# A float32 decoder trunk on one core: low halves of the feed-forward forms by accumulating DMAs, three more seven-product pairs per layer, one in each GLA projection, four pieces of work later

## The chip, the core and the metric

The kernel runs on one core of one Trainium2 chip. The engines named below are TensorE (PE, matrix products), VectorE (DVE), ScalarE (ACT), GpSimd (POOL) and SyncE (SP); each works through its own instructions in order, and DMA queues are started from SP, POOL and ACT. The metric is the device time of one execution in microseconds (us). A profiled execution takes 2254.6 us, of which its trace spans 2252.8.

## The reference, cut to what matters

256 tokens of width 2048, all float32. Two layers; each has a token mixer with a cross-attention beside it, an output projection and a feed-forward part:

```
mem_n = _rmsnorm(mem, norm_mem)
for layer in range(2):
    hn = _rmsnorm(h, norm_mix[layer])
    y, xq = mixer(hn, w_in)              # layer 0: HGRN2, layer 1: gated linear attention (GLA)
    xa = _memory_attention(xq, mem_n, w_mem_kv[layer])
    h = h + concatenate([y, xa]) @ w_out[layer]
    hn = _rmsnorm(h, norm_ffn[layer])
    gate, up = split(hn @ w_gate_up[layer])
    h = h + (silu(gate) * up) @ w_down[layer]
return _rmsnorm(h, norm_final)
```

## The kernel before, in words

**Halves.** Every float32 factor is split into a high half, rounded to the matmul's format, and a low half, the rest. A product of two blocks is three matmuls: high by high, high by low, low by high. The weights come from HBM into a buffer `raw`, one pair of rows of blocks at a time (256 rows, four quarters of up to 512 columns). ACT casts them into the high half and DVE subtracts that from the buffer for the low half; both halves lie in a tile `parts87c` and the like (the number counts the weight pairs, the letter the split in it; in output projection some are called `parts_0` and `parts_2`).

**Plain, seven and H pairs.** A pair joins a 2 by 2 grid of x blocks (two row blocks, two token halves of 128) with a 2 by 2 grid of weight blocks. Plain, it is eight block products, 24 matmuls, and two splits of 1024 columns each. With a Strassen-Winograd scheme it is seven products, 21 matmuls ("S"): sums of the weight quarters are formed in `raw` and split as well (function `seven`; splits a to d of 512, 1024, 1024 and 1024 columns), and sums of the x blocks ("s", "d0", "u", "z") are needed beside them. If it is fed, one of the quarter sums is made by an accumulating DMA of POOL (line 444 for `raw`, lines 428 and 429 for a tile `T` beside it). "H" and "O" are other forms with eight products, which need fewer or no sums: H splits 1024, 1024 and 512 columns and forms one difference of 512. A plan such as `0-1S2S3-` lists pairs and kinds in their order; KINDS lists the kinds of the eight pairs of a feed-forward block, its first entry for block 0 ("block one" below).

**Forms of x.** In the feed-forward part class `Forms` (line 371) makes the x side of a pair once per layer: PE transposes four blocks of h (`tp_hf`), ACT writes them with the gain into `g`, a buffer of a ring of two (tag "stg"; `hf_7g` for pair 7), DVE adds up the further forms in `g`, and `parts()` (line 402) makes the halves `hf_7h` and `hf_7l` (one tile `hf_6hl` for pair 6): an ACT copy and a DVE subtraction, 1024 columns for eight forms. Pair 7 is of kind "B": when that is done, a ninth form is written into g[:, 4] and split likewise. Class `More` makes the further forms for output projection and down projection from halves that exist (tiles `y_6g`, `y_6m`).

**The stages.** The memory tokens are projected to keys and values for both layers (`m0p`, `m1p`; scaling by the memory norm behind the first); then per layer the mixer, output projection (its first quarter alone, `wo`; quarters two and three by plan OUT; its last quarter alone), and eleven feed-forward blocks of 512 columns (`f_p`) with the down projection (`fd`) between them. GLA works in two halves (`pr` 0 and 1); each first projects keys and queries (`gk0p`, 384 columns wide, plan "------S-"), which ACT scales (`gsk`, `gsq`) and PE transposes (`tgk`, `tgq`), then gates and values (`gg00p`).

**What sets the order.** Small work (transposes, attention, scores) waits in a list; `later(...)` appends pieces, and one piece is taken out at marks between the matmuls of a projection, so that `None` in the list moves what follows by one mark. A scheduler then lists the instructions of each engine when the program is built; on the chip each engine keeps to its list. One helper line (L151) issues nearly all instructions, so the profile's rows are told apart by tiles.

Of the kernel before, what the change touches and what calls it, by code (L numbers as in the profile page):

```python
# [9 lines left out]
F32 = mybir.dt.float32  # L10
# [3 lines left out]
AF = mybir.ActivationFunctionType  # L14
# [26 lines left out]
def trunk_kernel(ctx: ExitStack, tc: tile.TileContext, x, mem, norm_mix, norm_ffn, norm_mem,  # L41
# [210 lines left out]
    def later(*pieces):  # L252
        pending.extend(pieces)
# [119 lines left out]
    class Forms:  # L373
# [20 lines left out]
        def put(self, ps, gains):  # L394

            g = work.tile([P, 8, P], F32, tag="stg", name=f"{self.name}g", bufs=2)
            for k in range(2):
                ac.activation(out=g[:, 2 * k:2 * k + 2, :], in_=ps[:, 2 * k * P:(2 * k + 2) * P].rearrange(
                    "p (a t) -> p a t", t=P), func=AF.Copy, scale=gains[k])
            tt = ve.tensor_tensor  # L400

            def parts(i, j, n):
                ac.copy(out=self.h[:, i:i + n, :], in_=g[:, j:j + n, :])
                tt(out=self.l[:, i:i + n, :], in0=g[:, j:j + n, :], in1=self.h[:, i:i + n, :].bitcast(F32), op=ALU.subtract)

            if self.kind == "O":
                tt(out=g[:, 4:6, :], in0=g[:, 1:3, :], in1=g[:, 0:4:3, :], op=ALU.subtract)
                parts(0, 0, 6)
                return
            tt(out=g[:, 4:6, :], in0=g[:, 3:0:-2, :], in1=g[:, 0:1, :].broadcast_to([P, 2, P]), op=ALU.subtract)  # L410
            ve.scalar_tensor_tensor(out=g[:, 6, :], in0=g[:, 3, :], scalar=-1.0, in1=g[:, 5, :],
                                    op0=ALU.mult, op1=ALU.subtract)
            tt(out=g[:, 7, :], in0=g[:, 2, :], in1=g[:, 6, :], op=ALU.add)
            parts(0, 0, 8)
            if self.kind == "B":
                tt(out=g[:, 4, :], in0=g[:, 2, :], in1=g[:, 3, :], op=ALU.subtract)
                parts(8, 4, 1)
# [256 lines left out]

    def h_quad(hq, q, gain, ss, name, queue=later, sevens=SEVEN):

# [11 lines left out]

        queue(turn)

# [85 lines left out]
    for l in range(2):  # L776
# [4 lines left out]
        project_two(memq["pairs"], MEM[l], w_mem_kv[l], 0, XA, XA, f"m{l}",  # L781
                    lambda: [lambda t: ks[:, t, :], lambda t: vm[l][:, t, :]], prep=prep_mem if l == 0 else None)
        if l == 0:
# [5 lines left out]
            for q in range(NQ):  # L789

                h_quad(hq, q, g_mix[0], ss, "hx", later if q > 1 else first_turns.append)
        for d in (ks, vm[l]):
            for t in range(NT):
                ac.activation(out=d[:, t, :], in_=d[:, t, :], func=AF.Copy, scale=rm[:, t:t + 1])

# [4 lines left out]

        later(turn_keys)

# [4 lines left out]
    def attention(l, ps, r, yq):  # L807
# [42 lines left out]
        def mix():  # L850
            quad = yq[3] = Quad("tq", f"y{l}_3")
            for j in range(2):
# [7 lines left out]

        later(turn_queries, None, lambda: softmax(0), lambda: softmax(1), None,
              lambda: turn_probs(0), lambda: turn_probs(1), mix)
# [204 lines left out]
    def gla_pair(w, pr, dec, decay, hq, r, yq):  # L1067
# [40 lines left out]
        def give():  # L1108
            for name in "kq":
# [3 lines left out]

        project_two(hq["pairs"], ("------S-", "------S-")[pr], w, kw + pr * 2 * DK, pr * 2 * DK, 2 * DK, f"gk{pr}", give,
                    lambda ps: ps.rearrange("p (a c) -> p a c", c=DK), fed=False)
# [5 lines left out]
        if pr == 0:  # L1121
            scores[5:5] = [lambda: decay(1), None]
        later(None, None, turn_k, turn_q, None, None, *scores)
        GLA = (("-----SS-", "-----SS-"), ("-----SS-", "-----SS-"))
# [71 lines left out]

    KINDS = ("SHHSHOSO", "HHHSSOSO", "SHHSSOSO", "SSHSSOHS", "SSSSSOSS")

# [112 lines left out]

    OUT = "4-5-2-0S6S7-3S1-"

# [3 lines left out]
    for l in range(2):  # L1317
# [33 lines left out]
        if l == 0:  # L1351
            hq = {}
            ffn(0, hq2, r2, lambda n: h_quad(hq, n, g_mix[1], ss, "hm1_", sevens=2))
            scale = lambda ss=ss: h_scale(ss, "rm1", True)
# [79 lines left out]
```

## Time and profile before

| | |
|---|---|
| Median of 3 runs | 2254.84 us (2254.82 to 2255.8) |
| The profiled execution | 2254.6 us |
| Its span in the trace | 2252.8 us |
| Busy: PE, DVE, ACT, POOL | 2238.6, 2031.5, 1452.8, 280.4 us |
| Granted TensorE clock, mean | 0.999 |
| DMA queue of POOL (software) | 25632 packets, 50.87 MB, 13.0% of 16 engines |
| DMA queue of SP (hardware) | 228547 packets, 420.21 MB, 55.5% |

The two times are to be kept apart: the profiled execution is 1.8 us longer than the span that its trace covers, and durations read from the trace belong to that one execution. A busy share is a mean over stages with different limits; what a stage is short of is read from the stretch of the trace that holds it. In a timeline, `[0.74 <-ACT parts88c]` after a row says that the engine stood idle for 0.74 us before it, and what ended that.

### The profile page before, as it was taken

The numbers are of one execution on the slowest core, as the hardware profiler recorded it, in microseconds if no ns is written. First come the engines' busy times: TensorE is split into PE (matmuls) and PEld (weight loads), VectorE is DVE, ScalarE is ACT, GpSimd is POOL, SyncE is SP. The second block draws the span as 40 slices with busy tenths as digits, with TensorE's granted clock in tenths as the row PEclk, the third lists the DMA queues.
The fourth block names the chain that finished last, engine by engine and source line by source line (L and its number), as shares of the span: only waits on it lengthen the run. The fifth ranks groups of instructions, "written<-read, shape, count | busy, mean of one in ns | idle before, by whom it ended". The sixth has DMA issues, their size and how long they took to land.

```text
span 2252.8 us, 30400 instructions
## 1 busy us (share of the span) xinstructions
PE 2238.6 (99%) x10668; PEld 1894.6 (84%) x10668; DVE 2031.5 (90%) x2551; ACT 1452.8 (64%) x2010; POOL 280.4 (12%) x275
## 2 busy tenths in 40 slices
PE   9999999999999999999999999999999999999998
PEld 7888888888888888888889999988888888888887
DVE  6879899898998999999996887889999999999997
ACT  7656656565666666666665665566566676666664
POOL 1000100000111112112210000000011221212110
PEclk9999999999999999999999999999999999999999
DMA  8656655656687778878865445566677878887874
GB/s 296 215 168 213 199 182 177 200 193 190 198 236 232 229 234 231 230 230 238 244 221 168 141 156 182 164 209 197 208 221 224 233 230 238 242 238 236 231 233 167
DMA packets 255628, 477.28 MB, mean 212 GB/s; under 512 B 18255, under 2 KB 47731, under 8 KB 255219
## 3 DMA queue, kind: packets, MB, share of 16 engines
q1 hardware_dynamic: 228547, 420.21, 55.5%
q0 software_dynamic: 25632, 50.87, 13.0%
q10 hardware_dynamic: 1296, 4.26, 0.5%
q8 instruction: 84, 1.38, 0.2%
q14 instruction: 69, 0.57, 0.1%
HBM read 472.12 MB, written 3.15 MB: 211 GB/s over the span
## 4 chain that ended last, share of the span: by engine, by line
PE 90%; DVE 6%; issue 2%; DMA 1%; ACT 1%; SPq 0%; POOL 0%; DVEq 0%; POOLq 0%; ACTq 0%
PE f_p L151 34%; PE fd L151 18%; PE wo L151 4%; PE m1p L151 2%; PE hv2p L151 2%; PE hv1p L151 2%; PE hf0p L151 2%; PE hv0p L151 2%; PE wo1p L151 2%; PE hf2p L151 2%; PE hf1p L151 2%; PE wo0p L151 2%; PE m0p L151 2%; PE gk0p L151 1%; PE gk1p L151 1%
## 5 line engine op out<-in xcount | busy, mean ns | idle before, releaser
L151 DVE TENSOR_TENSOR raw<-raw 128x1024 f32<-128x1024 f32 (+3 forms) x330 | 311.2, 943 | 16.7 <-DMA raw<-in_w_down_dram 5.6
L151 ACT CAST parts<-raw 128x1024 fp32r<-128x1024 f32 (+1 forms) x216 | 211.7, 1016 | 56.8 <-DMA raw<-in_w_down_dram 14.7
L151 DVE TENSOR_TENSOR parts<-raw,parts 128x1024 fp32r<-128x1024 f32 (+1 forms) x176 | 200.2, 1171 | 22.7 <-ACT parts L151 22.0
L444 POOL DMA_DIRECT2D raw<-in_w_gate_up_dram x92 | 80.4, 873 | 541.2 <-DMA raw<-in_w_gate_up_dram 274.7
L300 POOL TENSOR_TENSOR parts<-raw,parts 128x1024 fp32r<-128x1024 f32 x40 | 95.6, 2406 | 113.5 <-ACT parts L151 81.2
L151 ACT COPY h<-fd 128x512 f32<-128x512 f32 x80 | 45.7, 588 | 46.5 <-PE fd L151 44.0
L428 POOL DMA_DIRECT2D T<-in_w_gate_up_dram x36 | 21.1, 587 | 430.2 <-DVE hf_4g L151 82.7
L151 ACT ACTIVATE s<-s,rf_r 128x512 f32<-128x512 f32 x44 | 31.8, 723 | 42.0 <-DVE s L151 42.0
L151 DVE SCALAR_TENSOR_TENSOR s<-e,rf_r,s 128x512 f32<-128x512 f32 x44 | 45.7, 1076 | 2.9 <-ACT s L151 0.5
L151 DVE TENSOR_TENSOR e<-f_p,e 128x512 f32<-128x512 f32 x66 | 45.2, 684 | 2.6 <-DVE s L151 0.5
L429 POOL DMA_DIRECT2D T<-in_w_gate_up_dram x36 | 31.0, 861 | 120.4 <-DMA T<-in_w_gate_up_dram 111.1
L151 ACT COPY fd<-h 128x512 f32<-128x512 f32 x82 | 45.2, 582 | 0.0
L444 POOL DMA_DIRECT2D raw<-in_hgrn_w_in_dram x17 | 14.7, 867 | 209.9 <-DMA raw<-in_hgrn_w_in_dram 124.6
L151 PE MATMUL fd<-parts,s_0h 128*128 128x512 f32 x128 | 39.8, 392 | 0.0
L151 PE MATMUL fd<-parts,s_4h 128*128 128x512 f32 x128 | 39.8, 392 | 0.0
L151 PE MATMUL fd<-parts,s_8h 128*128 128x512 f32 x128 | 39.8, 392 | 0.0
L151 PE MATMUL fd<-parts,s_2h 128*128 128x512 f32 x128 | 39.8, 392 | 0.0
L151 PE MATMUL fd<-parts,s_6h 128*128 128x512 f32 x128 | 39.8, 392 | 0.0
L151 PE MATMUL fd<-parts,s_1h 128*128 128x512 f32 x128 | 39.4, 389 | 0.0
L151 PE MATMUL fd<-parts,s_3h 128*128 128x512 f32 x128 | 39.4, 389 | 0.0
L151 PE MATMUL fd<-parts,s_5h 128*128 128x512 f32 x128 | 39.4, 389 | 0.0
L151 PE MATMUL fd<-parts,s_7h 128*128 128x512 f32 x128 | 39.4, 389 | 0.0
(6020 smaller groups left out, 7434.0 us busy)
## 6 DMA issues: line engine op xcount, KB each, us to landing
raw<-in_w_gate_up_dram SPq DMA_DIRECT2D x224, 512.0 KB, 4.4
raw<-in_w_down_dram SPq DMA_DIRECT2D x80, 1024.0 KB, 5.5
raw<-in_w_gate_up_dram SPq DMA_DIRECT2D x220, 256.0 KB, 4.2
raw<-in_hgrn_w_in_dram SPq DMA_DIRECT2D x79, 512.0 KB, 4.6
raw<-in_gla_w_in_dram SPq DMA_DIRECT2D x96, 384.0 KB, 3.3
raw<-in_w_gate_up_dram POOLq DMA_DIRECT2D x92, 256.0 KB, 4.9
T<-in_w_gate_up_dram POOLq DMA_DIRECT2D x72, 256.0 KB, 5.0
raw<-in_w_out_dram SPq DMA_DIRECT2D x16, 1024.0 KB, 5.1
```

The source lines that it names most:

```text
L151: ins = func(*args, **kwargs)
L300: low = (nc.gpsimd if free_port else ve).tensor_tensor(out=both[:, 1, k:j, 0:m], in0=src[:, k:j, :], in1=both[:, 0, k:j, 0:m].bitcast(F32) ...
L428: nc.gpsimd.dma_start(out=both[:, 0, :], in_=rows[0])
L429: nc.gpsimd.dma_start(out=both[:, 0, :], in_=rows[1], accum_op=ALU.add)
L444: nc.gpsimd.dma_start(out=raw[:, 1, 0:n], in_=rows[1], accum_op=ALU.add)
```

## The change

1. `Forms.parts`: the low half is made as minus g by an ACT copy, and POOL issues an accumulating DMA that adds g to it, from one on-chip buffer to another; the DVE subtraction is gone. The DMA reads g, so whoever writes g next has to wait for it.
2. OUT: pair 7 of output projection becomes a seven, the fourth there (its x sums are made by `More`, as for 6, 3 and 1).
3. KINDS: in block one, pairs 2 and 4 go from H to S, in both layers.
4. The key and query projections of GLA have two sevens rather than one.
5. Later: the scaling of layer 0's memory keys and values goes behind the first weights of the next projection; their transposes two marks later; the transposes of layer 0's queries one mark; GLA's keys and queries of the first half two marks; the third quarter's transposes for the next mixer (`tp_hm`) one mark.

As built, PE has 10364 matmuls in place of 10388 (18 of 512 columns and 6 of 384 fewer), DVE has 10 more additions or subtractions and 10 more scaled ones, ACT 32 more instructions, POOL 24 more DMAs (18 for the forms, 6 for weights), SP 6 more.

```diff
--- before.py
+++ after.py
@@ -401,7 +401,8 @@
 
             def parts(i, j, n):
                 ac.copy(out=self.h[:, i:i + n, :], in_=g[:, j:j + n, :])
-                tt(out=self.l[:, i:i + n, :], in0=g[:, j:j + n, :], in1=self.h[:, i:i + n, :].bitcast(F32), op=ALU.subtract)
+                ac.activation(out=self.l[:, i:i + n, :], in_=g[:, j:j + n, :], func=AF.Copy, scale=-1.0)
+                nc.gpsimd.dma_start(out=self.l[:, i:i + n, :].bitcast(F32), in_=g[:, j:j + n, :], accum_op=ALU.add)
 
             if self.kind == "O":
                 tt(out=g[:, 4:6, :], in0=g[:, 1:3, :], in1=g[:, 0:4:3, :], op=ALU.subtract)
@@ -672,7 +673,7 @@
     MANY = 12
 
 
-    def h_quad(hq, q, gain, ss, name, queue=later, sevens=SEVEN):
+    def h_quad(hq, q, gain, ss, name, queue=later, sevens=SEVEN, wait=False):
 
         for t in range(NT):
             square_sum(h[:, t, q * 512:(q + 1) * 512], ss[:, t, q:q + 1], f"{name}{q}{t}")
@@ -686,7 +687,7 @@
             hq[q] = Pairs(*both)
             hq.setdefault("pairs", {}).update({2 * q: both[0], 2 * q + 1: both[1]})
 
-        queue(turn)
+        queue(*([None] if wait else []), turn)
 
     def h_forms(forms, n, gain, ss, name):
 
@@ -779,7 +780,7 @@
         vm.append(kv[:, 1, :].rearrange("p (m c) -> p m c", c=XA))
         ks = work.tile([P, NT, XA], F32, tag="stg", name=f"ks{l}", bufs=2)
         project_two(memq["pairs"], MEM[l], w_mem_kv[l], 0, XA, XA, f"m{l}",
-                    lambda: [lambda t: ks[:, t, :], lambda t: vm[l][:, t, :]], prep=prep_mem if l == 0 else None)
+                    lambda: [lambda t: ks[:, t, :], lambda t: vm[l][:, t, :]], prep=prep_mem if l == 0 else prep_last)
         if l == 0:
             later(*[lambda p=p: more_of(memq, p, "hq", f"mem{p}") for p in range(len(PAIRS))
                     if f"{p}S" in MEM[1] and f"{p}S" not in MEM[0]])
@@ -789,16 +790,22 @@
             for q in range(NQ):
 
                 h_quad(hq, q, g_mix[0], ss, "hx", later if q > 1 else first_turns.append)
-        for d in (ks, vm[l]):
-            for t in range(NT):
-                ac.activation(out=d[:, t, :], in_=d[:, t, :], func=AF.Copy, scale=rm[:, t:t + 1])
+        def scaled(l=l, ks=ks):
+            for d in (ks, vm[l]):
+                for t in range(NT):
+                    ac.activation(out=d[:, t, :], in_=d[:, t, :], func=AF.Copy, scale=rm[:, t:t + 1])
+
+        if l:
+            scaled()
+        else:
+            prep_last = lambda at: at == 1 and scaled()
 
         def turn_keys(l=l, ks=ks):
             for j in range(2):
                 tp = transposes([lambda t, c=2 * j + i: ks[:, t, c * P:(c + 1) * P] for i in range(2)], f"tk{l}{j}")
                 ve.tensor_copy(kT[l][:, 2 * j:2 * j + 2, :].rearrange("p h t -> p (h t)"), tp)
 
-        later(turn_keys)
+        later(*([None, None] if l == 0 else []), turn_keys)
 
     kv_out = away.tile([P, 2, XH * T], F32, name="kv_out")
     later(lambda: nc.scalar.dma_start(out=kv_out, in_=kv))
@@ -858,7 +865,7 @@
                                          st["pT", m][:, c, :], start=m == 0, stop=m == 1)
                 quad.put(2 * j, 2, op)
 
-        later(turn_queries, None, lambda: softmax(0), lambda: softmax(1), None,
+        later(*([None] if l == 0 else []), turn_queries, None, lambda: softmax(0), lambda: softmax(1), None,
               lambda: turn_probs(0), lambda: turn_probs(1), mix)
 
 
@@ -1111,7 +1118,7 @@
                 nc.gpsimd.memset(dst[-1][:, :, :, DK:T], 0.0)
             return [lambda t, d=d: d[:, t, :, 0:DK] for d in dst]
 
-        project_two(hq["pairs"], ("------S-", "------S-")[pr], w, kw + pr * 2 * DK, pr * 2 * DK, 2 * DK, f"gk{pr}", give,
+        project_two(hq["pairs"], "-----SS-", w, kw + pr * 2 * DK, pr * 2 * DK, 2 * DK, f"gk{pr}", give,
                     lambda ps: ps.rearrange("p (a c) -> p a c", c=DK), fed=False)
         for d in dst:
             for t in range(NT):
@@ -1120,7 +1127,7 @@
         scores = gated_scores(st, [[0, 1], [2, 3]], f"g{pr}")
         if pr == 0:
             scores[5:5] = [lambda: decay(1), None]
-        later(None, None, turn_k, turn_q, None, None, *scores)
+        later(*([None] * (2 if pr else 4)), turn_k, turn_q, None, None, *scores)
         GLA = (("-----SS-", "-----SS-"), ("-----SS-", "-----SS-"))
         gate, v = [], []
         for a in range(2):
@@ -1194,7 +1201,7 @@
     PARTS = ((0,), (1, 2), (3, 4), (5, 6), (7, 8), (9, 10))
 
 
-    KINDS = ("SHHSHOSO", "HHHSSOSO", "SHHSSOSO", "SSHSSOHS", "SSSSSOSS")
+    KINDS = ("SHSSSOSO", "HHHSSOSO", "SHHSSOSO", "SSHSSOHS", "SSSSSOSS")
 
 
 
@@ -1309,7 +1316,7 @@
 
     ENDS = (('0-1S2S3-',), ('0-1S2S3-',))
 
-    OUT = "4-5-2-0S6S7-3S1-"
+    OUT = "4-5-2-0S6S7S3S1-"
 
 
     flush()
@@ -1350,7 +1357,7 @@
         ss = new_ss(f"ss_n{l}")
         if l == 0:
             hq = {}
-            ffn(0, hq2, r2, lambda n: h_quad(hq, n, g_mix[1], ss, "hm1_", sevens=2))
+            ffn(0, hq2, r2, lambda n: h_quad(hq, n, g_mix[1], ss, "hm1_", sevens=2, wait=n == 2))
             scale = lambda ss=ss: h_scale(ss, "rm1", True)
         else:
             gf = []
```

How the order moves at the places where the forms are made, in layer 0. First ACT, from the copies of `hf_4g` out of the transposes on; 84c and the like are weight splits of block one. Before:

```order
L151 ACTIVATE hf_4g<-tp_hf_4_4265,pv 128x256
L151 CAST hf_3h<-hf_3g 128x1024
L151 ACTIVATE hf_4g<-tp_hf_4_4265,pv 128x256
L151 ACTIVATE parts84c<-T_0_4380 128x512
L151 ACTIVATE parts84c<-raw_4383 128x512
L151 ACTIVATE hf_5g<-tp_hf_5_4300,pv 128x256 x2
L151 CAST parts84d<-raw_4383 128x1024
L151 CAST hf_4h<-hf_4g 128x1024
L151 CAST hf_5h<-hf_5g 128x768
```

and now:

```order
L151 ACTIVATE hf_4g<-tp_hf_4_4285,pv 128x256 x2
L151 CAST parts84a<-raw_4405 128x512
L151 CAST parts84b<-raw_4405 128x1024
L151 ACTIVATE hf_5g<-tp_hf_5_4321,pv 128x256 x2
L151 ACTIVATE parts84c<-T_0_4402 128x512
L151 CAST hf_4h<-hf_4g 128x1024
L151 ACTIVATE hf_4l<-hf_4g 128x1024
L151 CAST hf_5h<-hf_5g 128x768
L151 ACTIVATE hf_5l<-hf_5g 128x768
L151 ACTIVATE parts84c<-raw_4405 128x512
L151 CAST parts84d<-raw_4405 128x1024
```

The negative copies of `hf_4l` and `hf_5l` are added, and those of `hf_2l` and `hf_3l` stand ahead of this piece. The casts of 84a and 84b now stand behind `hf_4g`; the halves of 84c stand apart.

ACT further on, from the high half of pair 6's forms to the cast of 87d (pair 87 is the fourth of block one). Before:

```order
L151 CAST hf_6hl<-hf_6g 128x1024
L151 CAST parts87a<-raw_4536 128x512
L151 ACTIVATE hf_7g<-tp_hf_7_4483,pv 128x256 x2
L151 CAST parts87b<-raw_4536 128x1024
L151 CAST hf_7h<-hf_7g 128x1024
L151 ACTIVATE parts87c<-raw_4536 128x1024
```

and now, to 87c:

```order
L151 CAST hf_6hl<-hf_6g 128x1024
L151 ACTIVATE hf_6hl<-hf_6g 128x1024
L151 ACTIVATE parts86c<-raw_4524 128x1024
L151 CAST parts86d<-raw_4524 128x1024
L151 ACTIVATE hf_7g<-tp_hf_7_4506,pv 128x256 x2
L151 CAST parts87a<-raw_4564 128x512
L151 CAST parts87b<-raw_4564 128x1024
L151 CAST hf_7h<-hf_7g 128x1024
L151 ACTIVATE hf_7l<-hf_7g 128x1024
L151 ACTIVATE parts87c<-raw_4564 128x1024
```

Pair 86 is a seven now and adds 86c of 1024 and 86d; the negative copies of `hf_6hl` and `hf_7l` stand ahead of the casts of 86c and 87c.

DVE, from pair 87's third split to pair 88's. Before (from the low half of `hf_7`, 1024 wide):

```order
L151 TENSOR_TENSOR hf_7l<-hf_7g,hf_7h 128x1024
L151 TENSOR_TENSOR raw_4536<-raw_4536 128x512
L151 TENSOR_TENSOR hf_7g<-hf_7g 128x128
L151 TENSOR_TENSOR raw_4536<-raw_4536 128x1024
L151 SCALAR_TENSOR_TENSOR parts87c<-raw_4536,parts87c 128x1024
L151 TENSOR_TENSOR hf_7l<-hf_7g,hf_7h 128x128
L151 TENSOR_TENSOR parts87d<-raw_4536,parts87d 128x1024
L151 TENSOR_TENSOR parts88a<-raw_4576,parts88a 128x1024
L151 TENSOR_TENSOR parts88b<-raw_4576,parts88b 128x1024
```

and now (`hf_7g` 128x128 is the ninth form of pair 7, which is written where the eight before were read):

```order
L151 SCALAR_TENSOR_TENSOR parts87c<-raw_4564,parts87c 128x1024
L151 TENSOR_TENSOR parts87d<-raw_4564,parts87d 128x1024
L151 TENSOR_TENSOR parts88a<-raw_4604,parts88a 128x512
L151 TENSOR_TENSOR hf_7g<-hf_7g 128x128
L151 TENSOR_TENSOR parts88b<-raw_4604,parts88b 128x1024
L151 TENSOR_TENSOR raw_4604<-raw_4604 128x512
L151 TENSOR_TENSOR raw_4604<-raw_4604 128x1024
L151 SCALAR_TENSOR_TENSOR parts88c<-raw_4604,parts88c 128x1024
L151 TENSOR_TENSOR parts88d<-raw_4604,parts88d 128x1024
```

The two subtractions into `hf_7l` are gone; the ninth form moved from ahead of 87c to between 88a and 88b, and pair 88, a seven now, has two sums in `raw` and the splits c and d of 1024.

## The prediction

> **What bounds the kernel now.** I read the page first, for span and engines; then the busy time by stretch, the waits of PE, and the timelines of PE, DVE and ACT where the change puts work. The page:
>
> ```profile
> span 2252.8 us, 30400 instructions
> PE 2238.6 (99%) x10668; PEld 1894.6 (84%) x10668; DVE 2031.5 (90%) x2551; ACT 1452.8 (64%) x2010; POOL 280.4 (12%) x275
> raw<-in_w_gate_up_dram SPq DMA_DIRECT2D x224, 512.0 KB, 4.4
> raw<-in_w_down_dram SPq DMA_DIRECT2D x80, 1024.0 KB, 5.5
> raw<-in_w_gate_up_dram SPq DMA_DIRECT2D x220, 256.0 KB, 4.2
> raw<-in_gla_w_in_dram SPq DMA_DIRECT2D x96, 384.0 KB, 3.3
> raw<-in_w_gate_up_dram POOLq DMA_DIRECT2D x92, 256.0 KB, 4.9
> ```
>
> TensorE (PE) is busy 99% of the span, so the time falls only if it gets fewer matmuls or waits less, and rises by each new wait. VectorE (DVE) stands at 90% on average; the stretches around the change tell more. Columns: window, its length, then busy us of PE, PEld, DVE, ACT and POOL, each with its number of instructions, granted clock, DMA share, GB/s.
>
> ```profile
> 443.50:462.50 19.00, 18.28 (x85) 14.65 (x85) 18.98 (x36) 11.97 (x20) 1.44 (x2) 1.00 0.53 142
> 462.50:480.00 17.50, 17.50 (x79) 14.45 (x78) 17.41 (x21) 11.97 (x14) 0.86 (x1) 1.00 0.61 194
> 480.00:493.20 13.20, 13.20 (x60) 10.94 (x59) 11.71 (x16) 7.93 (x10) 0.00 (x0) 1.00 0.70 238
> 530.00:545.00 15.00, 15.00 (x67) 12.20 (x66) 13.92 (x17) 9.25 (x11) 0.90 (x1) 1.00 0.42 121
> 1305.00:1320.00 15.00, 14.81 (x92) 14.49 (x91) 14.14 (x23) 11.75 (x16) 0.31 (x1) 1.00 0.52 169
> ```
>
> DVE is full in output projection (443.5 to 480), nearly full in the first feed-forward block (530 to 545) and in gated linear attention (GLA; 1305 to 1320). PE is fed there only as long as what DVE finished earlier lasts. The waits of PE (engine, tile and line, what was waited for, us in total, times, longest):
>
> ```profile
> PE tgk L151 <- ACT gsk L151: 1.4, 2, 0.8
> PE tp_hm L151 <- DVE h L151: 1.0, 2, 0.8
> PE m1p L151 <- ACT parts8a L151: 0.4, 1, 0.4
> PE f_p L151 <- DVE parts96c L151: 0.3, 1, 0.3
> PE tx L151 <- ACT xs L151: 0.2, 1, 0.2
> ```
>
> **What is saved.** A seven-product pair has 21 matmuls, a plain or an H pair 24. The fourth seven in output projection and the two in block one are three pairs in each of two layers, 18 matmuls 512 wide; the GLA key and query projections lose 6 that are 384 wide. Their pitch, from groups of PE's timeline:
>
> ```profile
> 549.85 1.52 PE L151 MATMUL f_p<-parts90b,hf_6hl 128*128 128x512 f32 x6
> 551.21 1.52 PE L151 MATMUL f_p<-parts90c,hf_6hl 128*128 128x512 f32 x6
> 1273.40 2.24 PE L151 MATMUL gk0p<-parts231b,hm_7x 128*128 128x384 f32 x12
> 1275.48 2.25 PE L151 MATMUL gg00p<-parts232a,hm_2x 128*128 128x384 f32 x12
> ```
>
> (551.21 - 549.85)/6 = 0.227 us and (1275.48 - 1273.40)/12 = 0.173 us; 18 x 0.227 + 6 x 0.173 = 5.1 us. The four pieces moved later are those that PE waits for: memory scaling (m1p 0.4), layer-0 queries (tx 0.2), GLA keys (tgk 1.4) and the third quarter's transposes (tp_hm 1.0): 3.0 us. GLA's transposes move behind 12 further matmuls (2.08 us), more than the two waits together. **Saved: 8.1 us**, if nothing new waits. The 3.0 could come back in part, as GLA's scores now start later in a stretch where DVE is busy 14.14 of 15 us: 0 to 1.4, and I take 0.
>
> **What it costs on DVE.** The durations, and the place that decides, are in DVE's timeline of the first feed-forward block (start, duration, tile, in brackets the idle time ahead):
>
> ```profile
> 524.30 0.28 DVE L151 TENSOR_TENSOR hf_6g<-hf_6g 128x128 f32<-128x128 f32 x1
> 525.76 1.23 DVE L151 TENSOR_TENSOR hf_6hl<-hf_6g,hf_6hl 128x1024 fp32r<-128x1024 f32 x1 [1.17 <-ACT hf_6hl L151]
> 528.31 0.69 DVE L151 TENSOR_TENSOR parts87a<-raw,parts87a 128x512 fp32r<-128x512 f32 x1 [1.32 <-ACT parts87a L151]
> 529.05 0.42 DVE L151 TENSOR_TENSOR hf_7g<-hf_7g 128x256 f32<-128x256 f32 x1
> 529.50 0.29 DVE L151 SCALAR_TENSOR_TENSOR hf_7g<-hf_7g 128x128 f32<-128x128 f32 x1
> 531.30 1.22 DVE L151 TENSOR_TENSOR hf_7l<-hf_7g,hf_7h 128x1024 fp32r<-128x1024 f32 x1
> 532.44 0.69 DVE L151 TENSOR_TENSOR raw<-raw 128x512 f32<-128x512 f32 x1
> 533.04 0.28 DVE L151 TENSOR_TENSOR hf_7g<-hf_7g 128x128 f32<-128x128 f32 x1
> 533.25 1.22 DVE L151 TENSOR_TENSOR raw<-raw 128x1024 f32<-128x1024 f32 x1
> 534.38 1.22 DVE L151 SCALAR_TENSOR_TENSOR parts87c<-raw,parts87c 128x1024 fp32r<-128x1024 f32 x1
> ```
>
> Start to start, a 1024-wide operation takes 1.14 us and a 512-wide one 0.60. An H pair costs DVE two splits of 1024 and two operations of 512, 3.5 us; a seven-product pair four of 1024 and two of 512, 5.8. Block one gains 2 x 2.3 = 4.6 us of DVE work and loses the eight low-half subtractions of the layer (hf_7l is one), 8 x 1.14 = 9.1 at most. By the sum DVE is relieved. But two of the eight lie ahead of block one in output projection (2.3), where a plain pair becomes a seven (5.8 less two splits of 1024, so 3.5 more) and its extra forms cost about 2.0 (two operations of 512 and four of 128). So 3.2 us net are added where DVE has 36.39 of 36.5 us and only 1.5 us free just after. What DVE has finished in advance covers most: I take 0.5 us of new waits per layer, bounds 0 and 3.2 - 1.5 = 1.7.
>
> **The place that decides: pairs 86 to 88.** ACT, PE and POOL there and a little ahead (start, duration, tile):
>
> ```profile
> 501.76 1.05 ACT L151 CAST hf_2h<-hf_2g 128x1024 fp32r<-128x1024 f32 x1 [0.30 <-DVE hf_2g L151]
> 502.71 1.05 ACT L151 CAST parts84b<-raw 128x1024 fp32r<-128x1024 f32 x1
> 504.64 0.48 ACT L151 ACTIVATE hf_4g<-tp_hf,pv 128x256 f32<-128x256 f32 x1 [0.88 <-DVE hf_2l L151]
> 524.68 1.05 ACT L151 CAST hf_6hl<-hf_6g 128x1024 fp32r<-128x1024 f32 x1 [1.17 <-DVE hf_6g L151]
> 530.21 1.06 ACT L151 CAST hf_7h<-hf_7g 128x1024 fp32r<-128x1024 f32 x1 [0.26 <-DVE hf_7g L151]
> 535.42 0.73 PE L151 MATMUL f_p<-parts87c,hf_3h 128*128 128x512 f32 x2
> 540.09 0.90 POOL L444 DMA_DIRECT2D raw<-in_w_gate_up_dram  x1 [18.87 <-DVE raw L151]
> ```
>
> DVE's split of 87c ends at 535.60 and PE starts on it at 535.42: no lead is left. The forms' chain sets the pace (transposes, ACT, DVE; the idle 1.17 and 1.32 above are it). An ACT copy of 1024 takes 0.95 start to start (502.71 - 501.76), so each negative copy adds that on ACT.
>
> *First wait.* I start the changed order where the last hf_6g ends as before, at 524.6. ACT casts hf_6's high half from 524.68, then makes the negative copy (to 526.7), then 86c, now 1024 wide (527.6). DVE splits 86c to 528.9 and 86d to 530.0, then takes hf_7g (0.45), 87a (0.60), hf_7g (0.21), 87b (1.14), hf_7g (0.28): 532.6. ACT's hf_7h, hf_7l and 87c, one behind another, end at 532.7 + 0.95 + 0.95 + 1.05 = 535.7, DVE's 87c at 537.0. PE is 3 matmuls earlier than before (535.42 - 0.7 = 534.7) and needs the low half one matmul later, at 534.95: 2.05 us. At least 1.1, if DVE reaches hf_7g right behind the transposes.
>
> *The DMA's price.* The trace has no 512 KB accumulation from SBUF. Nearest is the 256 KB accumulation of POOL's queue, 4.9 us; SP's rows grow by 0.2 (256 to 512 KB) and by 1.1 us (to 1024), so my estimate is 4.9 + 0.6 = 5.5; bounds 3.3 (the quickest row above) and 9.8 (4.9 twice).
>
> *The wait at hf_7g.* The fourth form of pair 7 overwrites a part of hf_7g that the accumulating DMA of hf_7l still reads, and DVE stands at this write with 88b, both raw sums, 88c and 88d queued behind it. The DMA follows ACT's hf_7l, at 534.75, and lands at 540.25; DVE ends 88b at 541.7. PE (from 537.0, 15 matmuls on) wants it at 540.4: 1.3 us. DVE then does both sums and 88c (0.60 + 1.14 + 1.22, to 544.6), while PE is there at 543.1: 1.5 us. With 3.3 us these are 0 and 1.2; with 7.5, 3.3 and 1.5.
>
> *The ring of g.* It has two buffers, so ACT's hf_4g must wait for the DMA of hf_2l, as it waited 0.88 us for DVE's hf_2l. hf_2h from 501.76, its negative copy to 503.75, landing at 509.25, where hf_4g ran at 504.64. Queued behind it on ACT stand 84a, 84b, hf_5g, half of 84c, the four copies of hf_4 and hf_5, and the other half of 84c: some 7.3 us with hf_4g, to 516.6. DVE's line from there to the last hf_6g (84c, 84d, two adds to h, 85a, 85b, 86b, a raw sum, 85c, the small ones) is some 8.9 us: 525.5 instead of 524.6. That moves the first wait by **0.8 us**; 0 with 3.3 us, 2.9 with 7.5.
>
> Together 2.05 + 1.3 + 1.5 + 0.8 = **5.7 us per layer**; 3.3 with the quick DMA, 9.8 with 7.5 us.
>
> The Trainium skill ("DMA: Bandwidth & Descriptors", section "Anatomy of one DMA — SWDGE (gpsimd) path") fits such a transfer as 2.0 us plus its bytes at 436 GB/s. It gives 2.6 us for 256 KB where this trace has 4.9, so the measurement decides; by the page 512 KB would take 3.2 us (an estimate from it), and the sum would be that of the quick DMA.
>
> The same order stands in layer 1 (pairs 290 to 292), so it counts twice. The later wait on 96c (0.3) I let grow by 0.4 per layer, as the added copies and DVE pairs lie ahead of it; bounds 0 and 1.2. In GLA a plain pair (two splits of 768) becomes a seven, some 3 us more DVE work where DVE still has room: 0.
>
> **Sum.** Per layer 0.5 + 5.7 + 0.4 = 6.6, twice 13.2; 13.2 - 8.1 = +5.1 us. The profiled execution took 2254.6 us (its span and 1.8 around it), 0.2 below the median 2254.84, so the forecast is **2259.7 us**. A measurement of this kernel can tell 0.2%, 4.5 us, from no change; the forecast lies just beyond.
>
> **The rivals.**
> *The relief wins* (faster): the forms' 9.1 us of DVE work per layer let DVE and ACT reach pair 86 early, and the waits at 87c, 88b and 88c shrink to some 1 us in all per layer: 2254.6 - 8.1 + 2 = 2248.5. For: PE waits for DVE in this stage, and the 5.1 us of matmuls are sure. Against: DVE idles ahead of hf_6hl and 87a, so it isn't DVE alone that is late there. It decides if all waits of a layer stay under 1.8 us. Chance 0.26.
> *The DMA is quick*: landing in 3.3 us, 2 x (0.5 + 3.3 + 0.4) = 8.4 against 8.1: 2254.9. For: 384 KB did so on SP's queue; against: no row of POOL's. Chance 0.12. To this time the skill's fit would lead.
> *The DMA is slow* (slower, far): with 7.5 us, 2 x (0.5 + 9.8 + 0.4) = 21.4 - 8.1 = +13.3: 2267.9. It decides from about 6.5 us; each further us costs 2 to 4. For: these DMAs queue one behind another on POOL, 0.90 us an issue, beside a DMA share of 0.42 to 0.70. At 9.8 us it would be some 2277, which I leave out. Chance 0.20.
> *The forecast*: waits of 4 to 8 us per layer at pairs 86 to 88, 2256.3 to 2264.3: chance 0.42, of which 0.17 within 0.2% and 0.25 above.
>
> **Numbers.** Faster 0.26; within 0.2%, 0.12 + 0.17 = 0.29; slower 0.25 + 0.20 = 0.45. The range 2247 to 2268 leaves out the best part of the first rival and the worst half of the third; the likeliest case alone is 2256.3 to 2264.3.
>
> **What would show it.** In the changed profile: 24 matmuls fewer; the waits on gsk, h, parts8a and xs gone; new rows PE f_p <- DVE parts87c, 88b and 88c (and 291c, 292b, 292c) of 1 to 3 us each; DVE idle ahead of the last hf_7g, released by the DMA of hf_7l, some 5.5 us after its issue; ACT idle ahead of hf_4g, released by that of hf_2l. I am wrong if f_p waits for none of these, if hf_7g's wait ends on ACT, or if GLA shows new waits of more than 1.4 us.

## The result, and the profile after

The changed kernel takes 2277.69 us (median of 5 runs, 2274.85 to 2279.45), the kernel before 2255.8 us (5 runs): a ratio of 1.0098, with a 95% interval of 1.0087 to 1.0108. It is 22 us slower. The forecast was 2259.7 us with a range up to 2268: the direction is right, the size isn't. The profiled execution is the slowest of the five, 2279.45 us, and its span is 24.9 us longer than before's. Its page:

```profile
span 2277.7 us, 30521 instructions
PE 2244.3 (99%) x10644; PEld 1890.9 (83%) x10644; DVE 2039.3 (90%) x2571; ACT 1477.4 (65%) x2042; POOL 302.1 (13%) x299
q0 software_dynamic: 29088, 60.70, 15.5%
```

PE has 24 matmuls fewer (10644 against 10668) and is busy 5.7 us longer: on average a matmul's record became longer. The waits of PE, as shown of before:

```profile
PE f_p L151 <- ACT parts84c L151: 3.0, 1, 3.0
PE f_p L151 <- ACT parts291c L151: 1.8, 1, 1.8
PE f_p L151 <- ACT parts87c L151: 1.7, 1, 1.7
PE f_p L151 <- DVE parts292b L151: 1.1, 1, 1.1
...
PE spg L151 <- DVE GQ L151: 1.1, 1, 1.1
PE slg L151 <- ACT ggate L151: 0.9, 1, 0.9
PE f_p L151 <- DVE parts87c L151: 0.8, 1, 0.8
...
PE f_p L151 <- DVE parts88c L151: 0.8, 1, 0.8
...
PE m1p L151 <- ACT parts8a L151: 0.4, 1, 0.4
```

The waits on gsk and on h are gone, as meant. In their place stand the waits at 84c, 87c, 88c and their like in layer 1, two new ones of GLA's scores (spg, slg), and the one on parts8a as before. Where the 24.9 us arise shows in the start of the first matmul of a weight pair, in PE's two timelines (us):

| first matmul of pair | place | before | after | later by |
|---|---|---|---|---|
| 74 | output projection, layer 0 | 462.3 | 462.8 | 0.6 |
| 84 | block one, layer 0 | 516.8 | 518.6 | 1.8 |
| 85 | | 521.9 | 529.1 | 7.2 |
| 87 | | 533.4 | 540.0 | 6.6 |
| 88 | | 538.3 | 549.4 | 11.1 |
| 89 | | 543.7 | 556.2 | 12.5 |
| 224 | mixer, layer 1 | 1231.5 | 1245.3 | 13.8 |
| 254 | end of GLA | 1384.4 | 1398.6 | 14.2 |
| 288 | block one, layer 1 | 1560.0 | 1574.5 | 14.5 |
| 293 | | 1587.0 | 1609.2 | 22.2 |
| end of the span | | 2252.8 | 2277.7 | 24.9 |

Two places of some 30 us each, block one of either layer, hold 18.4 of the 24.9 us. GLA, with its later pieces and its sevens, comes out about even. Another 2 us arise at pairs 139 to 141, where DVE waits 1.9 us for the DMA of a weight; why it lands late is not followed up here. What stands behind the first of these places is in ACT's timeline (start, duration, tile, idle time ahead and what ended it):

```profile
504.96 1.06 ACT L151 CAST hf_2h<-hf_2g 128x1024 fp32r<-128x1024 f32 x1
505.92 1.06 ACT L151 ACTIVATE hf_2l<-hf_2g 128x1024 fp32r<-128x1024 f32 x1
...
515.03 0.84 ACT L151 ACTIVATE hf_4g<-tp_hf,pv 128x256 f32<-128x256 f32 x2 [4.28 <-DMA hf_2l<-hf_2g]
```

ACT stands 4.28 us at hf_4g until the DMA of hf_2l has landed, with the casts of 84a, 84b and 84c queued behind it, and another 1.23 us at hf_5g for hf_3l; PE has then used up its weights and waits 3.05 us at 84c. The DMAs' rows (KB each, median us from issue to landing):

```profile
hf_1l<-hf_1g POOLq DMA_DIRECT2D x2, 512.0 KB, 8.1
hf_2l<-hf_2g POOLq DMA_DIRECT2D x2, 512.0 KB, 7.7
hf_3l<-hf_3g POOLq DMA_DIRECT2D x2, 512.0 KB, 9.2
hf_4l<-hf_4g POOLq DMA_DIRECT2D x2, 512.0 KB, 6.5
hf_6hl<-hf_6g POOLq DMA_DIRECT2D x2, 512.0 KB, 7.2
hf_7l<-hf_7g POOLq DMA_DIRECT2D x2, 512.0 KB, 5.6
```

The forecast had 5.5 us. Why they take so long is in the busy time by stretch (columns as in the prediction: the last but one is the DMA engines' busy share). Before, from 511 to 515 us:

```profile
511.00:515.00 4.00, 4.00 (x20) 3.30 (x19) 3.84 (x4) 2.56 (x4) 0.97 (x2) 1.00 0.71 231
```

and after:

```profile
511.00:515.00 4.00, 4.00 (x20) 3.30 (x19) 1.20 (x2) 0.00 (x0) 0.00 (x0) 1.00 1.09 274
```

By this share all 16 DMA engines are full while ACT does nothing. In the packets of the trace, those of hf_2l start at 511.0, 3.7 us after POOL's issue at 507.27. SP issues two loads of block one's weights 0.3 and 0.7 us behind POOL's issue, and their packets go first, slowly from 508 to 510 us:

```profile
508.00:509.00 1.00, 1.00 (x6) 0.84 (x5) 0.00 (x0) 1.00 (x2) 0.13 (x1) 1.00 0.89 61
509.00:510.00 1.00, 1.00 (x7) 0.81 (x6) 0.17 (x1) 1.00 (x2) 0.84 (x1) 1.00 0.43 45
```

Layer 1 has the same 3.7 us. Why the later load goes first, and why so little moves there (61 and 45 GB/s), isn't shown. Then a 4096-byte packet of the accumulation takes 327 ns, a 2048-byte packet of the weights 84 ns, so an accumulated byte takes about twice the time of a loaded one; by this estimate 128 packets of 4096 bytes hold all 16 engines for 128 x 0.327/16 = 2.6 us.

The second thing that the forecast lacked is in PE's granted clock, by the same view, behind the waits at 84c and at 87c:

```profile
523.80:528.80 5.00, 4.73 (x13) 3.49 (x14) 4.74 (x6) 4.97 (x8) 1.48 (x2) 0.66 1.00 201
...
545.50:547.00 1.50, 1.50 (x5) 1.15 (x4) 1.36 (x2) 0.77 (x1) 0.00 (x0) 0.50 1.09 223
547.00:548.50 1.50, 1.50 (x5) 1.19 (x4) 0.00 (x0) 0.00 (x0) 0.00 (x0) 0.50 0.88 229
```

Behind each of these two places (waits of 3.05 us; of 1.73 and 0.76 us) PE gets half the clock for 3.41 us, so here a wait costs more than its length. From 60 us on, the clock falls nowhere else before the last matmul: behind 1.84 and 0.76 us at 291c in layer 1 it stays at 1.00:

```profile
1597.00:1605.00 8.00, 5.61 (x21) 3.79 (x21) 5.82 (x7) 4.13 (x7) 2.40 (x3) 1.00 0.98 277
```

Over the whole trace, from 60 us on: PE's idle time ahead of its matmuls adds up to 4.0 us before and 20.8 after; what the distance to the next start exceeds the usual 0.227, 0.173 or 0.109 us (512, 384 or 128 columns), idle time taken off, to 20.3 and 30.9 us. So 16.8 us of new waits, 10.6 us of longer distances and 1.8 us more behind the last matmul (7.1 and 8.9) stand against 5.1 us of matmuls saved: 24.1 of the 24.9. The half clock is the smaller part of the 10.6: about 3.3 us lie in its two stretches. About 5.1 us lie right ahead of recorded waits (39 of them, 13 before) and belong to these: idle time is counted from the end of a matmul's record, 0.39 us behind its start, and not from the 0.227 us at which the next one usually starts.

The Trainium skill ("TensorE: Matmul & The Clock Gate", section "Why this matters for your kernels") warns of idle gaps over about 3 us between matmuls, behind which the clock goes back to half. This trace agrees on the half (0.50) and, at 84c, on the gap (3.05 us); at 87c 1.73 and 0.76 us within 3 us were enough, at 291c 1.84 and 0.76 us were not.

### The profile page after: what moved, and what is told of

Read it like the earlier page. It is cut to its first block, busy times and chain, and to the rows that moved or that the text cites. A ratio compares the mean times of both kernels' runs of the same rounds, so it can differ in the third digit from the quotient of the medians.

```text
span 2277.7 us, 30521 instructions
## 1 busy us (share of the span) xinstructions
PE 2244.3 (99%) x10644; PEld 1890.9 (83%) x10644; DVE 2039.3 (90%) x2571; ACT 1477.4 (65%) x2042; POOL 302.1 (13%) x299
## 5 line engine op out<-in xcount | busy, mean ns | idle before, releaser
L151 DVE TENSOR_TENSOR raw<-raw 128x1024 f32<-128x1024 f32 (+2 forms) x344 | 324.0, 942 | 23.1 <-DMA raw<-in_w_down_dram 5.2
L151 ACT CAST parts<-raw 128x1024 fp32r<-128x1024 f32 (+1 forms) x216 | 211.3, 1016 | 52.0 <-DMA raw<-in_w_down_dram 15.6
```

The lines of the kernel that those rows point to most:

```text
L151: ins = func(*args, **kwargs)
```

## The experiments

Theory A: the loss is the latency of the forms' DMAs, behind which ACT (at hf_4g, by the ring of two buffers g) and DVE (at hf_7g) stand. Rival B: it is DVE's work for the new sevens. All times are medians; each is compared with runs of the kernel before made beside it (medians 2254.55 to 2255.76 us).

**Undo or do one part alone.** The changed kernel with the old low halves:

```diff
-                ac.activation(out=self.l[:, i:i + n, :], in_=g[:, j:j + n, :], func=AF.Copy, scale=-1.0)
-                nc.gpsimd.dma_start(out=self.l[:, i:i + n, :].bitcast(F32), in_=g[:, j:j + n, :], accum_op=ALU.add)
+                tt(out=self.l[:, i:i + n, :], in0=g[:, j:j + n, :], in1=self.h[:, i:i + n, :].bitcast(F32), op=ALU.subtract)
```

> The changed kernel with the old low halves: DVE subtracts again, no accumulating DMA for the forms; the sevens, GLA's and the later pieces stay. Theory A (the loss of 22 us is the latency of the forms' DMAs, behind which ACT at hf_4g and DVE at hf_7g stand, 6 to 9 us each): the waits at 84c, 85, 87c, 88b and their like in layer 1 go, and the time is 2250 to 2257, at least 20 us under the changed kernel. Rival B (the loss is DVE work of the new sevens, and the DMAs only take some of it off): with 9 us more DVE work per layer it gets slower than the changed kernel, 2280 or more.

Measured 2261.71 us, ratio 1.0031 (1.0020 to 1.0043): 16 us under the changed kernel. B is refuted as the cause of the whole: 9 us more DVE work per layer made it faster. But 6.5 us of loss remain, more than A gave. The reverse, the kernel before with only this edit of `parts()` put in:

> The kernel before with the low halves by accumulating DMAs and nothing else of the change. Theory A: slower by 12 to 22 us (2268 to 2278), with ACT idle some 4 us ahead of hf_4g and DVE some 2 us ahead of the last hf_7g. Rival B: DVE loses 9 us of work per layer, so the time is 2248 to 2256.

2259.32 us, 1.0017 (1.0008 to 1.0026): only 4 us. In the trace 2.3 us of these lie ahead of pair 74, before the first of the DMAs, where both kernels are the same. Here the DMA's wait is mostly covered: ACT idles 1.84 us ahead of hf_4g, 84a, 84b and 84c are cast before it, and PE has no wait between 460 and 560 us. A's number for this run was too high: the latency costs only where the casts of the next weights stand behind it. B's was too low: the relief of DVE gained nothing. Then the later pieces alone (part 5 of the change):

> The kernel before with the four pieces moved later and nothing else. The prediction's term: 3.0 us saved (2252.8) and PE's waits on gsk, h, parts8a and xs gone. Rival: only the wait on h goes (about 1 to 1.5 us: 2254.5), since the changed kernel still waits 0.4 us for parts8a and gives GLA's gain back at slg and spg.

2256.49 us, 1.0005 (0.9996 to 1.0014): no change. Its waits in GLA:

```profile
PE spg L151 <- DVE GQ L151: 2.4, 1, 2.4
...
PE slg L151 <- ACT ggate L151: 0.9, 1, 0.9
...
PE pxg L151 <- DVE GQ L151: 0.6, 1, 0.6
```

The 1.4 us on gsk are gone, and 3.9 us wait for the scores that now come later. And the three sevens per layer with low halves by DVE:

```diff
-    KINDS = ("SHHSHOSO", "HHHSSOSO", "SHHSSOSO", "SSHSSOHS", "SSSSSOSS")
+    KINDS = ("SHSSSOSO", "HHHSSOSO", "SHHSSOSO", "SSHSSOHS", "SSSSSOSS")
-    OUT = "4-5-2-0S6S7-3S1-"
+    OUT = "4-5-2-0S6S7S3S1-"
```

> The kernel before with the fourth seven in output projection and the two in block one, low halves by DVE as before. 18 matmuls fewer are worth 4.1 us. Theory A: their DVE work (5.5 us in output projection, 4.6 in block one, per layer) brings waits of 1 to 4 us per layer, so 2254 to 2260. Rival B: DVE runs dry, waits of 8 us or more per layer, 2268 or more.

2261.62 us, 1.0027 (1.0017 to 1.0038): 6 us slower, a little over A's range. As much as remained in the first run. The parts don't add up: about 4 us for the DMAs, 1 for the later pieces, 6 for the sevens, and 22 for all.

**Which wait.** The changed kernel, pairs 2 and 3 by DVE, so that no DMA holds g when hf_4g and hf_5g want it (`self.p` is the pair's number, kept by another line):

```diff
...
+                if self.p in (2, 3):
+                    tt(out=self.l[:, i:i + n, :], in0=g[:, j:j + n, :], in1=self.h[:, i:i + n, :].bitcast(F32), op=ALU.subtract)
+                    return
```

> The changed kernel, but the low halves of pairs 2 and 3 of the feed-forward forms are subtracted by DVE again, so that no DMA holds the two buffers of g when ACT copies hf_4g and hf_5g. Theory A (latency behind which engines stand): ACT's 4.3 us ahead of hf_4g go, PE's wait at 84c with it (5.4 us lost between pairs 84 and 85 in layer 0, about 2 in layer 1): 2268 to 2272. Rival B (DVE load): four subtractions more, 4.6 us of DVE work, so 2278 to 2283.

2267.75 us, 1.0056 (1.0043 to 1.0069): 10 us under the changed kernel. PE no longer waits at 84c. What is left is the other place, first in DVE's timeline, then PE's, then the clock behind it:

```profile
541.67 0.29 DVE L151 TENSOR_TENSOR hf_7g<-hf_7g 128x128 f32<-128x128 f32 x1 [3.86 <-DMA hf_7l<-hf_7g]
```

```profile
543.16 0.50 PE L151 MATMUL f_p<-parts88b,hf_4h 128*128 128x512 f32 x1 [3.31 <-DVE parts88b L151]
```

```profile
543.20:548.20 5.00, 4.54 (x13) 3.11 (x14) 4.93 (x5) 4.21 (x5) 1.35 (x2) 0.66 0.48 73
```

PE catches up with DVE, which stands 3.86 us for hf_7l: the step that the prediction called the wait at hf_7g, 3.31 us here, and a mean clock of 0.66 over the 5 us behind it. Next, that wait alone taken away, with the ring's left (`True` has DVE subtract, by a new argument of `parts`):

```diff
...
-            parts(0, 0, 8)
+            if self.kind == "B":
+                parts(0, 0, 4)
+                parts(4, 4, 4, True)
+            else:
+                parts(0, 0, 8)
...
-                parts(8, 4, 1)
+                parts(8, 4, 1, True)
```

> The changed kernel, but of pair 7 the DMA makes only the low halves of forms 0 to 3; DVE subtracts for forms 4 to 8, so that the ninth form's write no longer waits for a DMA. Theory A: DVE's 2.3 us ahead of the last hf_7g go, and 1.5 to 3 us per layer: 2272 to 2275. Rival B: 0.8 us more DVE work per layer, so 2277.7 or 1 to 2 us more.

2272.28 us, 1.0075 (1.0061 to 1.0088): 5.4 us under the changed kernel, as A has it; B fails again. Both edits together:

> The changed kernel with both edits of the two runs before together: pairs 2 and 3 by DVE, and of pair 7 only forms 0 to 3 by a DMA, so that no engine stands behind a form's DMA on the way to a weight split. Theory A (an engine standing behind a DMA is the loss): both savings add, 2256 to 2260, and it comes out under the kernel with all low halves by DVE (2261.7), as part of the relief of DVE is left. Rival C (the DMAs cost by filling the 16 DMA engines, and delay the weights whoever waits): 2262 to 2268.

2262.11 us, 1.0029 (1.0017 to 1.0040). The two savings add (10 + 5.4 = 15.4; measured 15.6), so the two waits with what follows them are worth 15.6 of the 21.9 us; the 6.4 that are left are as much as the three sevens alone lose. But the result is that of all low halves by DVE (2261.71): what DVE is relieved of by the DMAs that are left is worth nothing, and A's 2256 to 2260 is missed. Rival C's range holds the number; its reason, late weights, isn't shown by it, since the kernel without DMAs stands at the same time. PE's waits at 87c in this run:

```profile
536.06 0.51 PE L151 MATMUL f_p<-parts87c,hf_3h 128*128 128x512 f32 x1 [0.69 <-ACT parts87c L151]
537.45 0.50 PE L151 MATMUL f_p<-parts87c,hf_3h 128*128 128x512 f32 x1 [0.88 <-DVE parts87c L151]
```

and the clock behind them:

```profile
539.00:540.50 1.50, 1.50 (x5) 1.13 (x5) 1.50 (x3) 0.00 (x0) 0.00 (x0) 0.50 0.46 98
```

Two waits under 1 us each, within 2 us, stand ahead of a clock of 0.50 here.

**What makes the DMA slow.** The changed kernel without the addition (the low halves are then a copy of g, so this part of the computation is left out):

```diff
-                nc.gpsimd.dma_start(out=self.l[:, i:i + n, :].bitcast(F32), in_=g[:, j:j + n, :], accum_op=ALU.add)
+                nc.gpsimd.dma_start(out=self.l[:, i:i + n, :].bitcast(F32), in_=g[:, j:j + n, :])
```

> The changed kernel with the forms' DMAs as plain copies of g instead of accumulations: the same bytes, issues and waits, but nothing is added, so the low halves are wrong. In the trace of the changed kernel a 4096-byte packet of the accumulation takes 327 ns and a 2048-byte packet of the weights 84 ns. If the doubled time of an accumulating packet is what makes the DMA land late, hf_2l to hf_7l land 1 to 2.5 us earlier and the time is 2264 to 2272. If the landing is set by issue and by the weights queued ahead, it stays at 2275 to 2279.

2263.96 us, 1.0041 (1.0028 to 1.0053): 13.7 us under the changed kernel, with DMAs of the same number and size and the same waits on them. The DMAs land sooner, ACT hardly waits for the first of them, and the stretch moves more bytes:

```profile
hf_2l<-hf_2g POOLq DMA_DIRECT2D x2, 512.0 KB, 4.0
hf_3l<-hf_3g POOLq DMA_DIRECT2D x2, 512.0 KB, 6.5
```

```profile
510.72 0.84 ACT L151 ACTIVATE hf_4g<-tp_hf,pv 128x256 f32<-128x256 f32 x2 [0.41 <-DMA hf_2l<-hf_2g]
```

```profile
511.00:515.00 4.00, 4.00 (x20) 3.30 (x19) 3.41 (x6) 2.01 (x4) 0.00 (x0) 1.00 1.02 355
```

355 GB/s where the accumulation let 274 through, at full engines. A 4096-byte packet of the copy takes 159 ns, where one of the accumulation takes 327. And the copy's first packet comes 1.1 us after POOL's issue, not 3.7, though SP issues its loads 0.3 and 0.7 us behind it here too. So the accumulation is the price, and more of it lies ahead of the first packet (2.6 us of hf_2l's 3.7) than in the packets. Why an accumulation starts so late isn't shown; its issue takes POOL 0.86 us, that of a copy 0.53.

**Why all together cost more than the parts.** The changed kernel without block one's sevens:

```diff
-    KINDS = ("SHSSSOSO", "HHHSSOSO", "SHHSSOSO", "SSHSSOHS", "SSSSSOSS")
+    KINDS = ("SHHSHOSO", "HHHSSOSO", "SHHSSOSO", "SSHSSOHS", "SSSSSOSS")
```

> The changed kernel with the kinds of block one as before (H again in pairs 2 and 4); the DMAs, output projection's fourth seven, GLA's and the later pieces stay. 12 matmuls more cost 2.7 us. Theory A: the ring's wait at hf_4g stays (5.4 and 2 us), the waits at pairs 86 to 88 shrink to about 1 us per layer: 2268 to 2272. Rival B (block one's DVE work is the cause): 2258 to 2262.

2272.83 us, 1.0075 (1.0063 to 1.0088): 4.9 us under the changed kernel. A's mechanism with a little more loss than it had; B, which had 2258 to 2262, fails. And without the fourth seven of output projection:

```diff
-    OUT = "4-5-2-0S6S7S3S1-"
+    OUT = "4-5-2-0S6S7-3S1-"
```

> The changed kernel with output projection's plan as before (three sevens, 3 matmuls per layer more, 1.4 us in all). Theory A: its DVE work brings 1 to 2 us of waits per layer, so 2275 to 2277. Rival D (it makes the forms of pairs 2 and 3 late, and with them the wait at hf_4g): 2266 to 2272.

2265.61 us, 1.0049 (1.0036 to 1.0061): 12 us, as rival D has it. ACT and POOL of this run:

```profile
501.87 1.05 ACT L151 CAST hf_2h<-hf_2g 128x1024 fp32r<-128x1024 f32 x1 [0.30 <-DVE hf_2g L151]
...
509.50 0.84 ACT L151 ACTIVATE hf_4g<-tp_hf,pv 128x256 f32<-128x256 f32 x2 [1.74 <-DMA hf_2l<-hf_2g]
```

```profile
504.18 0.86 POOL L405 DMA_DIRECT2D hf_2l<-hf_2g  x1 [33.30 <-ACT hf_2l L151]
```

Without that seven the forms of pair 2 are made 3.1 us sooner (501.87 against 504.96), their DMA lands in 5.2 us and not 7.7, and hf_4g runs at 509.50 and not 515.03. PE's wait at 84c is gone. The first packet of hf_2l comes 1.5 us after its issue, although the engines are full of weights at that time (share 1.04, 399 GB/s); SP issues no load behind it until 512.61. So weights issued earlier are not enough to explain the 3.7 us of the changed kernel.

**Is anything left that is faster?** Two sevens in GLA's key and query projections and the third quarter's transposes later (`h_quad` as in the change), on the kernel before:

```diff
-        project_two(hq["pairs"], ("------S-", "------S-")[pr], w, kw + pr * 2 * DK, pr * 2 * DK, 2 * DK, f"gk{pr}", give,
+        project_two(hq["pairs"], "-----SS-", w, kw + pr * 2 * DK, pr * 2 * DK, 2 * DK, f"gk{pr}", give,
-            ffn(0, hq2, r2, lambda n: h_quad(hq, n, g_mix[1], ss, "hm1_", sevens=2))
+            ffn(0, hq2, r2, lambda n: h_quad(hq, n, g_mix[1], ss, "hm1_", sevens=2, wait=n == 2))
```

> The kernel before with two sevens in the GLA key and query projections and the third quarter's transposes one mark later, nothing else: the two parts of the change that the traces so far show to save. 6 matmuls of 384 are 1.0 us, the transposes' wait 1.5: 2252.7. Rival (the sevens' DVE work in GLA takes back what they save): 2253.8 or more.

2255.58 us, 1.0001 (0.9992 to 1.0009): no difference that can be told. With block one's sevens (the KINDS of the change) and the DMAs of the run with both waits taken away added:

> The kernel before with what the runs so far leave standing: block one's two sevens, two sevens in GLA's key and query projections, the third quarter's transposes one mark later, and accumulating DMAs for the low halves of pairs 0, 1, 4, 5, 6 and of pair 7's forms 0 to 3 (2 and 3 and the rest of 7 by DVE). 2.7 + 1.0 us of matmuls and 1.5 of a wait saved; if the relief of DVE covers block one's sevens, 2250 to 2254; if they still run dry at 87c and 88c, 2255 to 2259.

2261.19 us, 1.0025 (1.0015 to 1.0035): slower, and above both ranges, with 0.9 us at 87c by DVE, 0.4 by ACT, and 0.8 at 88c. No version beat the kernel before. So each seven alone, on the kernel before, one line a run:

```diff
-    KINDS = ("SHHSHOSO", "HHHSSOSO", "SHHSSOSO", "SSHSSOHS", "SSSSSOSS")
+    KINDS = ("SHSSHOSO", "HHHSSOSO", "SHHSSOSO", "SSHSSOHS", "SSSSSOSS")
...
+    KINDS = ("SHHSSOSO", "HHHSSOSO", "SHHSSOSO", "SSHSSOHS", "SSSSSOSS")
...
-    OUT = "4-5-2-0S6S7-3S1-"
+    OUT = "4-5-2-0S6S7S3S1-"
```

> The kernel before with one more seven in block one, pair 2 alone (kinds SHSSHOSO); 6 matmuls fewer, 1.4 us. If the loss of the sevens sits at pair 87, behind the added splits of pair 86 on DVE and ACT, this one brings waits of 2 to 3 us per layer at 87c: 2258 to 2260. If it comes from the sum of DVE work over the block, a third of it: 2256 to 2258.

> The kernel before with one more seven in block one, pair 4 alone (kinds SHHSSOSO); 6 matmuls fewer, 1.4 us. If pair 87 is the place, this one lies behind it, where PE has waited already, and costs little: 2254 to 2256. If it is the sum of DVE work, as much as pair 2 alone: 2256 to 2258.

> The kernel before with the fourth seven in output projection alone; 6 matmuls fewer, 1.4 us. The prediction took 0.5 us of waits per layer: 2255.2. In the traces so far some 0.9 to 1.8 us per layer are lost there: 2256 to 2258.

Measured 2255.88 us (1.0004, 0.9995 to 1.0013), 2258.26 us (1.0016, 1.0007 to 1.0025) and 2257.99 us (1.0014, 1.0006 to 1.0023). Pair 2 is even, under both of its ranges; pair 4 and output projection lose 3 to 4 us each, and pair 4 is above both of its ranges. The place that I had named, pair 87, is wrong as the sole place: behind pair 4's seven PE waits 0.8 us at 88c in either layer, behind output projection's 0.8 us at 282c in layer 1. In the trace of pair 4 block one of the two layers holds only 1.2 of the 3.7 us; where the rest arises isn't shown. Each saves 1.4 us of matmuls and spends that or more; their sum, 8.5 against 6 for all three, is within what the intervals allow. That the sum of DVE work decides rather than the place is not shown either, since pair 2 and pair 4 add the same work.

## Why the prediction was wrong, point by point

- **What bounds the kernel, and the direction**: right. PE was the bound, no lead was left in block one, and the loss came there, in both layers.
- **Saved by fewer matmuls, 5.1 us**: right, 24 fewer in the trace.
- **Saved by the later pieces, 3.0 us**: wrong. The wait on parts8a stayed, and GLA gave back 3.9 us for 1.4 (the later pieces alone: 1.0005). Only the transposes of the third quarter gained, some 1.6 us in the starts of pair 224. "0 to 1.4, and I take 0" was the wrong end. One sign of being wrong that the prediction names came true here: the changed kernel's GLA has 2.4 us of new waits (spg and slg), more than 1.4.
- **The first wait, 2.05 us at 87c**: right as a wait, and by the path described (hf_7h, hf_7l and 87c one behind another on ACT): 1.73 + 0.76 in layer 0, 1.8 + 0.8 in layer 1. What it cost, 4.5 us from pair 87 to 88 in layer 0, holds 2.0 us that no step had, most of it half clock (3.41 us at 0.50).
- **The DMA's price, 5.5 us**: right for hf_7l (5.6), too low for the others. I took it from a 256 KB accumulation out of HBM and let it grow as SP's plain loads do. The runs put 5.6 to 9.2 us in its place, 7.7 for hf_2l; the plain copy shows that the accumulation makes the difference (4.0 us for hf_2l, and 13.7 us of time). The bound of 9.8 us was in the text with its 2277 us, and was left out of the range. The fit of the Trainium skill (3.2 us, an estimate by its page "DMA: Bandwidth & Descriptors", section "Anatomy of one DMA — SWDGE (gpsimd) path") was further off.
- **The ring of g, 0.8 us per layer**: the step that failed. ACT does stand at hf_4g until hf_2l has landed, but I followed the delay only to the last hf_6g, where it was to move the first wait. PE already stands at 84c, whose cast is queued behind hf_4g: 3.05 us, and 5.4 us lost between pairs 84 and 85 in layer 0, half clock included, 1.8 between 288 and 289 in layer 1. With what it moves the ring is worth 10 us for both layers (the run with pairs 2 and 3 by DVE) in place of 1.6. hf_4g ran at 515.03 and not at 509.25, for two reasons: the DMA's price, 7.7 for 5.5, and hf_2h, which I let start at 501.76 as before. Output projection's seven makes that 504.96; without that seven the time falls by 12 us.
- **The wait at hf_7g, 1.3 + 1.5 us**: right in kind, and DVE idled 2.27 us there. The run that takes it away gains 5.4 us for both layers, about the 5.6 of the sum, but that agreement is partly luck: in layer 0 PE hardly waits at 88b (0.14 us), as it is late already from 84c and 87c. With the ring's wait gone it stands there for 3.3 and 2.9 us, more than the 1.3 of the sum.
- **Output projection, 0.5 us per layer; block one's own sevens**: too low. The three sevens alone cost 6 us net (1.0027), so some 10 us of waits and what follows them against 4.1 us of matmuls; the terms that hold them, 0.5 and 2.05 per layer, come to 5.1.
- **The rivals**: "the relief wins" is refuted, since with no wait left on a DMA the kernel is as slow as with DVE's subtractions. "The DMA is slow" was the nearest case; at the 7.5 us that it named, close to what was measured for hf_2l, it gave 2267.9, since it, too, had hf_2h at its old start, no wait at 84c, the 3.0 us of savings and no half clock.

The forecast missed by 18.0 us. By the runs that change one part each, the ring accounts for some 8.4 of these (10 for 1.6), the later pieces for about 3, the sevens for about 5 (10 for 5.1).

## What to carry to other kernels

Moving work from a full engine to a DMA pays only if nobody stands behind that DMA: look for the ring that hands its buffer on and for the next write to what it reads, and see which casts are queued behind them on an in-order engine. An accumulating DMA in a stage whose DMA engines already carry the weights is not free: here it took nearly twice as long to land as a plain copy (7.7 and 4.0 us). And ask at each delay for the first place at which the bounding engine needs the result, here 84c and not 87c. Where PE has no lead, a wait can bring half the clock behind it, here 3.41 us at 0.50 behind two waits, some 3.3 of the 24.9 us.

## What the runs showed of the hardware that I had not expected

- PE's granted clock fell to 0.50 for 3.41 us after waits of 1.73 and 0.76 us (the changed kernel at 87c), and after waits of 0.69 and 0.88 us within 2 us (both waits on DMAs taken away). It stayed at 1.00 after 1.84 and 0.76 us (the changed kernel at 291c) and after 0.85 and 0.89 us (291c in the combined run of 2261.19 us). What decides isn't shown.
- A 4096-byte packet of an accumulation from one on-chip buffer to another takes 327 ns, of a plain copy in its place 159 ns, a 2048-byte packet of a weight load 84 ns. Four us with accumulations moved 274 GB/s, with plain copies in their place 355 GB/s, both with full engines.
- The first packet of an accumulating DMA can come long after its issue: that of hf_2l came 3.7 us after it in both layers, with SP's loads issued 0.3 and 0.7 us behind it served first (layer 0), against 1.1 us for a plain copy at the same distance to SP's loads, and 1.5 us without output projection's fourth seven, where no load is issued right behind it.
